# Who copies the triangular blocks: GpSimd alone, or VectorE and GpSimd

## The chip, the cores and the metric

One core of a Trainium2 chip runs the whole kernel; the seven others are idle. The metric is the device time of one execution in microseconds (us). The engines are PE (TensorE, with its weight loads as PEld), DVE (VectorE), ACT (ScalarE), POOL (GpSimd) and SP (SyncE, which issues the DMAs). Each runs its own list of instructions in order, and they wait for each other through semaphores.

## The reference

One layer of a streaming encoder over 1024 tokens of width 1024: a projection, four mixers side by side (gMLP, gated deltanet, rwkv7, a conformer convolution), an output projection, a gated feed-forward block and a gate by position. Everything is in float32. Two of the mixers are recurrences over time. The deltanet is written in chunks of 64 tokens and solves a triangular system in each:

```python
L = jnp.where(strict, jnp.einsum('bhnid,bhnjd->bhnij', kb, k) * decay, 0.0)
eye = jnp.eye(CHUNK, dtype=jnp.float32)
rhs = jnp.concatenate([v * beta[..., None], kb * jnp.exp(g)[..., None]], axis=-1)
sol = lax.linalg.triangular_solve(eye + L, rhs, left_side=True, lower=True)
```

The rwkv mixer is a recurrence token by token:

```python
sa = jnp.einsum('bhij,bhj->bhi', state, a_t)
state = (state * w_t[:, :, None, :] + sa[..., None] * b_t[:, :, None, :]
         + v_t[..., None] * k_t[:, :, None, :])
```

## The kernel before

Tokens lie in 8 tiles of 128 (two chunks of 64), and each mixer has 4 heads. The kernel brings the rwkv recurrence to the same chunked form as the deltanet, so both need the inverses of 64 (8 tiles x 2 chunks x 4 heads) unit triangular matrices of 64x64. The matrices of all tiles are inverted together, and that splits each mixer's work into three stages.

**Pass 1** (`deltanet_pass1`, `rwkv_pass1`) makes the triangular matrices tile by tile. In the deltanet a tile goes from PE through ACT and DVE into the SBUF tile `la` (L736), in rwkv from PE through one ACT copy for each half of the heads into `LT` (L1027), of which there are two buffers. Then `compact` copies the blocks of that tile out: the four diagonal 32x32 blocks, one in each group of 32 partitions, into `Cd` (`rCd` for rwkv, L1179), with the tile's number innermost, and the two blocks beside the diagonal into `Mo` (`rMo`, L1182). That is four copies and two copies of 32 partitions x 128 elements for a tile, all on POOL. The names `Cd`, `la`, `Mo` of the profile belong to the deltanet, `rCd`, `LT`, `rMo` to rwkv.

**Inversion.** When all 8 tiles have been copied, DVE transposes `Cd` into `Cs` (L741; `rCs`, L1031) and runs a substitution of 31 steps over all blocks at once (`invert`, L216 and L220), about 118 small DVE instructions. `blocks` then transposes the result twice (`Tc`, `Tn`, L1135 and L1137), and PE multiplies the blocks together (L1146, L1148).

**Tile loop.** The tiles are solved and the states carried on (`deltanet_tiles`, `rwkv_tiles`). At its start `expand` spreads the inverted blocks over a block matrix with copies of the same shape (L1190, L1192), for the first tile on DVE, for the others on POOL.

Around these stages PE has work that doesn't depend on them: during the deltanet's inversion the projections of the rwkv inputs (`rwkv_in`, L136, taken out by ACT at L190 and DVE at L195), during rwkv's pass 1 the last of those projections and two sums (L1007, which DVE multiplies at L1008), during rwkv's inversion the output projection of two finished mixers (`wout_early`, L136 with `osph` and `ospl`). DVE and ACT prepare that work's operands: a weight is cast by ACT (`wh`, L109) and its rest subtracted by DVE (`wl`, L112).

The order on each engine is set when the kernel is built: a scheduler places the instructions by priorities that the code sets and by modelled times. The order is then fixed.

Of the kernel before, what the change touches and what calls it, by code (L numbers as in the profile page):

```python
# [97 lines left out]
class Net:  # L98
# [591 lines left out]
    def deltanet_pass1(self, ip):  # L690
        tc, nc, I = self.tc, self.nc, self.i
        V, A, PO = nc.vector, nc.scalar, nc.gpsimd
        beta, nbeta, gr, Gc, nG, eG, beG, edk, tmp, tmp2 = [self.bsc[:, j, :] for j in range(10)]
        fl = lambda x: x.rearrange("p a b -> p (a b)")
        inv = lambda n: self.dt(n, [P, 32, 32])
        Cd = inv("Cd")
        Mo = [ip.tile([P, 16, 32], F32, name=f"Mo{g}") for g in range(2)]
        rs = self.brs
        cc = [slice(0, 64), slice(64, 128)]
        for t in range(NT):  # L700
            qt, kt = self.qt[t // 4][:, t % 4, :], self.kt[t // 4][:, t % 4, :]
            for x, r0 in ((qt, 0), (kt, 4)):
                xv = x.rearrange("p (h d) -> p h d", d=64)
                PO.tensor_tensor(out=xv, in0=xv, in1=rs[:, t, r0:r0 + 4, None].broadcast_to([P, H, 64]), op=ALU.mult)
            ps = self.mps("b")
            for pr in range(2):
                nc.tensor.transpose(ps[:, (2 * pr) * P:(2 * pr + 1) * P], kt[:, pr * P:(pr + 1) * P], self.ident)
                nc.tensor.transpose(ps[:, (2 * pr + 1) * P:(2 * pr + 2) * P], qt[:, pr * P:(pr + 1) * P], self.ident)
            kq = self.at("kq", [P, 4, P])
            A.copy(out=kq.rearrange("p a b -> p (a b)"), in_=ps)  # L710
            pd = self.mps("c")[:, 0:256].rearrange("p (h i) -> p h i", h=H)
            nc.tensor.matmul(pd, self.identb, self.negb[:, None, :].broadcast_to([P, H, 64]), start=True, stop=False)
            for h in range(H):
                for c in cc:
                    nc.tensor.matmul(pd[c, h, :], gr[:, t * 4 + h:t * 4 + h + 1].broadcast_to([P, 64]), self.incl[:, c],
                                     start=False, stop=h == H - 1)
            dq = self.at("dq", [P, 4, G])
            dT = dq[:, 0, :].rearrange("p (h i) -> p h i", h=H)
            V.tensor_tensor(out=dT, in0=pd, in1=nG[:, 4 * t:4 * t + 4, None].broadcast_to([P, H, 64]), op=ALU.add)
            A.activation(out=dT, in_=dT, func=AF.Exp)  # L720
            qe, qeT = dq[:, 1, :], dq[:, 2, :]
            PO.tensor_tensor(out=qe.rearrange("p (h d) -> p h d", d=64), in0=qt.rearrange("p (h d) -> p h d", d=64),
                             in1=eG[:, 4 * t:4 * t + 4, None].broadcast_to([P, H, 64]), op=ALU.mult)
            pq = self.mps("b")
            for pr in range(2):
                nc.tensor.transpose(pq[:, pr * P:(pr + 1) * P], qe[:, pr * P:(pr + 1) * P], self.ident)
            A.copy(out=qeT, in_=pq[:, 0:256])
            nc.sync.dma_start(out=self.d_qe[:, t, :], in_=qeT)
            la = self.at("la", [P, 2, H, 64])
            for hp in range(2):  # L730
                pk = self.mps("c").rearrange("p (r k i) -> p r k i", r=2, k=4)[:, :, 0:2, :]
                rw = slice(64 * hp, 64 * hp + 64)
                for pr in range(2):
                    for c in cc:
                        nc.tensor.matmul(pk[c, pr], kq[rw, 2 * pr, c], kq[rw, 2 * pr:2 * pr + 2, c], start=True, stop=True)
                V.tensor_tensor(out=la[:, :, hp::2, :].rearrange("p k r i -> p r k i"), in0=pk,  # L736
                                in1=dT[:, hp::2, None, :].broadcast_to([P, 2, 2, 64]), op=ALU.mult)
            nc.sync.dma_start(out=self.d_at[:, t, :], in_=la[:, 1].rearrange("p h i -> p (h i)"))
            self.compact(Cd, Mo, la[:, 0], t)
        Cs = inv("Cs")  # L740
        V.transpose(out=fl(Cs), in_=fl(Cd))  # L741
        bt = ip.tile([P, 32], F32, name="bt")
        V.transpose(out=bt, in_=beta)
        V.tensor_tensor(out=Cs, in0=Cs, in1=bt[:, :, None].broadcast_to([P, 32, 32]), op=ALU.mult)
        X = self.invert(inv, Cs, 1)
        return self.blocks(inv, X, Mo, ip.tile([P, 32, 32], F32, name="Tc"), nbeta, "bc")
# [265 lines left out]
    def rwkv_pass1(self, eA, bk):  # L1012
        nc, V = self.nc, self.nc.vector
        inv = lambda n: self.at2(n, [P, 32, 32])
        Cd = inv("rCd")
        Mo = [self.ip.tile([P, 16, 32], F32, name=f"rMo{g}") for g in range(2)]
        for t in range(NT):
            LT = self.ar.tile([P, H, 64], F32, name="LT", tag="LT", bufs=2)
            for hp in range(2):
                rw = slice(64 * hp, 64 * hp + 64)  # L1020
                pa = self.mps("a")[:, 0:P].rearrange("p (r i) -> p r i", r=2)
                for pr in range(2):
                    for c in range(2):
                        o = t * P + 64 * c
                        nc.tensor.matmul(pa[64 * c:64 * c + 64, pr, :], bk[pr][rw, t, 3 * c, :], eA[pr][rw, o:o + 64],
                                         start=True, stop=True)
                nc.scalar.copy(out=LT[:, hp::2, :], in_=pa)  # L1027
            self.compact(Cd, Mo, LT, t)
        fl = lambda x: x.rearrange("p a b -> p (a b)")
        Cs = inv("rCs")  # L1030
        V.transpose(out=fl(Cs), in_=fl(Cd))  # L1031
        X = self.invert(inv, Cs, -1)
        return self.blocks(inv, X, Mo, self.ip.tile([P, 32, 32], F32, name="rTc"), None, "ac")
# [137 lines left out]
            nc.vector.tensor_copy(out=outs[1].rearrange("p a b c -> p (a b c)"), in_=pU[64:128])  # L1171
        yield

    def compact(self, Cd, Mo, LT, t):
        PO = self.nc.gpsimd
        for b in range(4):
            bs = slice(32 * b, 32 * b + 32)
            o = 32 * (b % 2)
            PO.tensor_scalar(out=Cd[bs, :, 4 * t:4 * t + 4].rearrange("p i u -> p u i"), in0=LT[bs, :, o:o + 32],  # L1179
                             scalar1=1.0, scalar2=0.0, op0=ALU.mult, op1=ALU.add)  # L1180
        for c in range(2):
            PO.tensor_scalar(out=Mo[t // 4][64 * c:64 * c + 32, 4 * (t % 4):4 * (t % 4) + 4, :], in0=LT[64 * c:64 * c + 32, :, 32:64],  # L1182
                             scalar1=1.0, scalar2=0.0, op0=ALU.mult, op1=ALU.add)
# [456 lines left out]
```

## Time and profile before

| | us |
|---|---|
| median of 3 runs | 1516.09 (1514.38 to 1516.21) |
| the profiled execution's own time | 1511.95 |
| its span, first to last instruction | 1509.9 |
| PE busy | 1397.1 |
| DVE busy | 1022.3 |
| ACT busy | 606.2 |
| POOL busy | 499.6 |

The profiled execution lies 4.14 us under the median of the runs, and 2.05 us of its time lie outside the span. PE is busy 93% of the span, so an engine beside it matters where PE waits for it. Busy time of PE also depends on the clock that it was granted (PEclk, as a share of full speed). A wait is listed with the engine whose instruction ended it. The timeline puts neighbouring instructions of the same kind into one row (x4), whose duration is then that of all of them.

### The profile page before, as it was taken

The page shows a single profiled execution, that of the slowest core. Times are in us where ns is not written, and L with a number is a line of the kernel's source. Part 1 is how long each engine was busy: PE and PEld are TensorE (multiplying, and loading weights), DVE is VectorE, ACT ScalarE, POOL GpSimd, SP SyncE. Part 2 cuts the span into 40 slices and gives each one's busy share as a digit, 9 for nine tenths or more (in the row PEclk, how much of TensorE's full clock was granted, in tenths as well). Part 3 has the DMA queues.
Part 4 walks back from the last instruction along what each step waited for, and adds up shares of the span by engine and source line. Part 5 has one row for each costly group of instructions (what it writes and reads, how often), then busy time and mean ns, then how long its engine had stood idle before and what let it go on. Part 6 is the DMA issues. An engine that isn't in the chain of part 4 may idle for free.

```text
span 1509.9 us, 21011 instructions
## 1 busy us (share of the span) xinstructions
PE 1397.1 (93%) x7840; PEld 1112.8 (74%) x7840; DVE 1022.3 (68%) x1714; ACT 606.2 (40%) x998; POOL 499.6 (33%) x484
## 2 busy tenths in 40 slices
PE   7997998899996898998789999999999899998997
PEld 6885776677764676776667888888888778876785
DVE  5699853976565757667488676666665695777543
ACT  6352355122542233345453333333333334445535
POOL 3215236262335233123522222222221354574000
PEclk9997999989998799999899999999999999999999
DMA  6100113132144343223444332222233893373022
GB/s 218 61 29 28 60 52 127 56 89 60 56 171 147 107 137 106 71 94 133 145 144 171 105 103 91 91 92 94 97 103 110 268 308 110 102 259 126 27 99 97
DMA packets 91735, 171.76 MB, mean 114 GB/s; under 512 B 12401, under 2 KB 41713, under 8 KB 91377
## 3 DMA queue, kind: packets, MB, share of 16 engines
q1 hardware_dynamic: 91344, 169.93, 34.0%
q8 instruction: 61, 1.00, 0.3%
q10 hardware_dynamic: 288, 0.49, 0.1%
q14 instruction: 42, 0.34, 0.1%
HBM read 120.85 MB, written 49.55 MB: 113 GB/s over the span
## 4 chain that ended last, share of the span: by engine, by line
PE 42%; DVE 4%; issue 3%; DMA 3%; POOL 2%; ACT 1%; SPq 0%; DVEq 0%; POOLq 0%; ACTq 0%
PE pf L136 39%; DMA w<-in_wd 2%; POOL wl L1215 1%; PE mps L136 1%; PE px L136 1%; DVE w L1211 1%; DVE wl L1215 0%; PE pf L1556 0%; DVE t L1211 0%; DVE nxn L151 0%; DMA d_f<-fo 0%; DMA early<-in_wd 0%; DVE s L1211 0%; POOL t L1211 0%; DVE ys L1211 0%
## 5 line engine op out<-in xcount | busy, mean ns | idle before, releaser
L136 PE MATMUL mps<-hT,wh 128*128 128x512 f32 (+1 forms) x736 | 242.5, 409 | 4.2 <-DVE mix L195 2.5
L136 PEld LDWEIGHTS mps<-hT,wh 128*128 128x128 f32 x736 | 141.2, 198 | 37.9 <-DVE mix L195 2.9
L136 PE MATMUL mps<-hT,wl 128*128 128x512 f32 (+1 forms) x368 | 149.5, 406 | 3.2 <-POOL wl L112 3.2
L1215 POOL TENSOR_TENSOR wl<-yr,wh 128x512 fp32r<-128x512 f32 x73 | 106.4, 1463 | 99.6 <-ACT wh L1214 81.7
L136 PE MATMUL pf<-wh 128*128 128x512 f32 x300 | 118.4, 395 | 4.2 <-ACT wh L1214 4.2
L112 POOL TENSOR_TENSOR wl<-raw,wh 128x1024 fp32r<-128x1024 f32 x25 | 64.7, 2592 | 173.1 <-ACT wh L109 173.1
L136 PE MATMUL pf<-wl,wh 128*128 128x512 f32 x300 | 118.7, 396 | 3.3 <-DVE wl L1215 3.3
L136 PE MATMUL pf<-wh,wl 128*128 128x512 f32 x300 | 117.9, 393 | 0.0
L1211 DVE TENSOR_TENSOR pf<-pf,u 128x512 f32<-128x512 f32 x88 | 61.1, 694 | 70.9 <-PE pf L136 70.8
L1214 ACT CAST fq<-s 128x512 fp32r<-128x512 f32 x88 | 53.5, 620 | 121.6 <-PE pf L136 96.5
L1215 POOL TENSOR_TENSOR fq<-raw,fq 128x512 fp32r<-128x512 f32 (+1 forms) x31 | 50.2, 1620 | 153.9 <-ACT fq L1214 153.9
L1215 DVE TENSOR_TENSOR wl<-w,wh 128x512 fp32r<-128x512 f32 x62 | 70.3, 1140 | 40.7 <-ACT wh L1214 40.7
L567 DVE SCALAR_TENSOR_TENSOR cy<-csg,prmt,cy 128x1023 f32<-128x1023 f32 (+29 forms) x60 | 86.4, 1461 | 7.2 <-ACT cy L564 6.6
L1215 POOL TENSOR_TENSOR wl<-raw,wh 128x1024 fp32r<-128x1024 f32 (+1 forms) x17 | 40.4, 2378 | 142.1 <-issue 116.0
L136 PEld LDWEIGHTS mps<-hT,wl 128*128 128x128 f32 x368 | 72.3, 196 | 19.9 <-POOL wl L112 3.7
L1214 ACT CAST wh<-yr 128x512 fp32r<-128x512 f32 x73 | 45.1, 620 | 81.3 <-POOL wl L1215 49.2
L136 PEld LDWEIGHTS pf<-wl,wh 128*128 128x128 f32 x300 | 57.1, 190 | 17.7 <-DVE wl L1215 6.0
L136 PEld LDWEIGHTS pf<-wh 128*128 128x128 f32 x300 | 57.1, 191 | 16.6 <-ACT wh L1214 4.6
L1215 DVE TENSOR_TENSOR fq<-s,fq 128x512 fp32r<-128x512 f32 x66 | 45.6, 693 | 30.7 <-ACT fq L1214 30.7
L136 PEld LDWEIGHTS pf<-wh,wl 128*128 128x128 f32 x300 | 57.0, 190 | 11.7
L136 PE MATMUL pf<-xT2h,fq 128*128 128x512 f32 x176 | 60.1, 403 | 5.3 <-ACT fq L1214 5.3
L109 ACT CAST wh<-raw 128x1024 fp32r<-128x1024 f32 x30 | 31.4, 1046 | 72.6 <-PE mps L136 38.5
(484 smaller groups left out, 3619.8 us busy)
## 6 DMA issues: line engine op xcount, KB each, us to landing
yr<-d_y SPq DMA_DIRECT2D x73, 256.0 KB, 3.1
w<-in_wd SPq DMA_DIRECT2D x55, 256.0 KB, 4.2
raw<-in_wg SPq DMA_DIRECT2D x24, 512.0 KB, 3.7
raw<-in_wu SPq DMA_DIRECT2D x24, 512.0 KB, 3.5
raw<-in_win SPq DMA_DIRECT2D x22, 512.0 KB, 3.8
d_y<-fy SPq DMA_DIRECT2D x11, 512.0 KB, 3.5
d_y<-ys SPq DMA_DIRECT2D x11, 512.0 KB, 3.5
d_y<-ys SPq DMA_DIRECT2D x22, 256.0 KB, 3.9
```

Source lines behind the costliest of these rows:

```text
L109: self.nc.scalar.copy(out=hi, in_=raw)
L112: (eng or self.nc.vector).tensor_sub(out=lo, in0=raw, in1=hi.bitcast(F32))
L136: mm = lambda *a, **k: self.nc.tensor.matmul(*a, skip_group_check=more, **k)
L567: nc.vector.scalar_tensor_tensor(out=yc[:, sh:], in0=gl[:, 0:S - sh], scalar=self.prm("cfw", 2 * j + c), in1=yc[:, sh:], op0=ALU.mult, op1 ...
L1211: eng.tensor_tensor(out=out, in0=a, in1=b, op=op)
L1214: self.nc.scalar.copy(out=hi, in_=raw)
L1215: eng.tensor_sub(out=lo, in0=raw, in1=hi.bitcast(F32))
```

## The change

`compact` gets a number `nv`. The first `nv` of the four diagonal copies go to DVE, the others stay on POOL. The deltanet passes 2, rwkv passes 4. The copies beside the diagonal stay on POOL in both.

```diff
--- before.py
+++ after.py
@@ -736,7 +736,7 @@
                 V.tensor_tensor(out=la[:, :, hp::2, :].rearrange("p k r i -> p r k i"), in0=pk,
                                 in1=dT[:, hp::2, None, :].broadcast_to([P, 2, 2, 64]), op=ALU.mult)
             nc.sync.dma_start(out=self.d_at[:, t, :], in_=la[:, 1].rearrange("p h i -> p (h i)"))
-            self.compact(Cd, Mo, la[:, 0], t)
+            self.compact(Cd, Mo, la[:, 0], t, 2)
         Cs = inv("Cs")
         V.transpose(out=fl(Cs), in_=fl(Cd))
         bt = ip.tile([P, 32], F32, name="bt")
@@ -1025,7 +1025,7 @@
                         nc.tensor.matmul(pa[64 * c:64 * c + 64, pr, :], bk[pr][rw, t, 3 * c, :], eA[pr][rw, o:o + 64],
                                          start=True, stop=True)
                 nc.scalar.copy(out=LT[:, hp::2, :], in_=pa)
-            self.compact(Cd, Mo, LT, t)
+            self.compact(Cd, Mo, LT, t, 4)
         fl = lambda x: x.rearrange("p a b -> p (a b)")
         Cs = inv("rCs")
         V.transpose(out=fl(Cs), in_=fl(Cd))
@@ -1171,12 +1171,12 @@
             nc.vector.tensor_copy(out=outs[1].rearrange("p a b c -> p (a b c)"), in_=pU[64:128])
         yield
 
-    def compact(self, Cd, Mo, LT, t):
+    def compact(self, Cd, Mo, LT, t, nv):
         PO = self.nc.gpsimd
         for b in range(4):
             bs = slice(32 * b, 32 * b + 32)
             o = 32 * (b % 2)
-            PO.tensor_scalar(out=Cd[bs, :, 4 * t:4 * t + 4].rearrange("p i u -> p u i"), in0=LT[bs, :, o:o + 32],
+            (self.nc.vector if b < nv else PO).tensor_scalar(out=Cd[bs, :, 4 * t:4 * t + 4].rearrange("p i u -> p u i"), in0=LT[bs, :, o:o + 32],
                              scalar1=1.0, scalar2=0.0, op0=ALU.mult, op1=ALU.add)
         for c in range(2):
             PO.tensor_scalar(out=Mo[t // 4][64 * c:64 * c + 32, 4 * (t % 4):4 * (t % 4) + 4, :], in0=LT[64 * c:64 * c + 32, :, 32:64],
```

The scheduler places the moved copies, and a few neighbours move with them. On DVE, in rwkv's pass 1, from the last rwkv inputs to the start of the inversion (`mix_4092` and `mix_4156` are the two halves of the product of L1008, `mix_4284` and `mix_4320` two rwkv inputs):

```order
-L1008 TENSOR_TENSOR mix_4092<-mps,mix_4284 128x512 x2
+L1008 TENSOR_TENSOR mix_4092<-mps,mix_4284 128x512
+L1179 TENSOR_SCALAR rCd<-LT 32x4x32 x8
+L1008 TENSOR_TENSOR mix_4092<-mps,mix_4284 128x512
+L1179 TENSOR_SCALAR rCd<-LT 32x4x32 x4
 L1008 TENSOR_TENSOR mix_4156<-mps,mix_4320 128x512
 L112 TENSOR_TENSOR wl<-raw,wh 128x1024
+L1179 TENSOR_SCALAR rCd<-LT 32x4x32 x20
 L1031 STREAM_TRANSPOSE rCs<-rCd 128x1024
 L205 MEMSET X 128x1024
-L112 TENSOR_TENSOR wl<-raw,wh 128x1024
 L195 SCALAR_TENSOR_TENSOR mix_4320<-mps,prmt,mix_4320 128x511
```

The 32 copies stand between the first product of L1008 and the transpose, and the copies of tiles 3 to 7 stand behind the weight's L112. One `wl` has moved behind L195.

On ACT, in the same place:

```order
 L190 ACTIVATE mix_4284<-mps,omu 128x512
 L1027 COPY LT<-mps 128x2x64 x6
+L109 CAST wh<-raw 128x1024
+L1027 COPY LT<-mps 128x2x64 x2
 L1009 ACTIVATE mix_4092<-mix_4092,prmt 128x1024
-L109 CAST wh<-raw 128x1024
-L1027 COPY LT<-mps 128x2x64 x10
+L1027 COPY LT<-mps 128x2x64 x8
```

The cast of the weight that DVE's L112 takes now stands ahead of the copies of tile 3 and ahead of L1009.

On POOL, in the deltanet's pass 1, one tile (L722 makes the scaled queries `dq` of a later tile):

```order
 L722 TENSOR_TENSOR dq<-qt_1114,bsc 128x256 x2
-L1179 TENSOR_SCALAR Cd<-la 32x4x32 x4
+L1179 TENSOR_SCALAR Cd<-la 32x4x32 x2
 L1182 TENSOR_SCALAR Mo_1796<-la 32x128 x2
 L722 TENSOR_TENSOR dq<-qt_1114,bsc 128x256
```

Two of the four copies have left POOL's list, the rest of the list is in its old order. On DVE the two copies stand right behind the two L736 that write `la`, ahead of the next tile's L719.

## Rows read from the trace of the kernel before

**Rows 1.** Page, part 1: busy us, share of the span, instructions.
```profile
PE 1397.1 (93%) x7840; PEld 1112.8 (74%) x7840; DVE 1022.3 (68%) x1714; ACT 606.2 (40%) x998; POOL 499.6 (33%) x484
```

**Rows 2.** Busy us by stretch: length, PE, PEld, DVE, ACT, POOL, then PEclk, DMA, GB/s.
```profile
236.60:260.20 23.60, 20.62 (x286) 14.47 (x285) 8.27 (x21) 10.55 (x23) 20.61 (x52) 1.00 0.36 122
...
448.00:469.50 21.50, 14.46 (x135) 8.82 (x135) 2.97 (x5) 7.97 (x21) 17.86 (x46) 0.76 0.49 176
...
475.30:515.00 39.70, 31.44 (x122) 24.04 (x121) 38.02 (x131) 10.38 (x21) 12.97 (x5) 0.89 0.47 157
```

**Rows 3.** Waits, 447 to 476: who <- whom, us in total, times, longest.
```profile
DVE rCs L1031 <- POOL rCd L1179: 14.7, 1, 14.7
ACT LT L1027 <- POOL rMo L1182: 11.6, 6, 3.0
...
PE mps L1025 <- ACT LT L1027: 5.8, 5, 2.4
```

**Rows 4.** Timeline of PE: start, us, instructions [idle before <- releaser].
```profile
297.58 1.20 PE L1146 MATMUL mps<-Tn,Mo 32*32 32x32 f32 x64 [3.02 <-DVE Tn L1137]
...
473.60 0.80 PE L136 MATMUL mps<-wh,osph 128*128 128x512 f32 x1 [4.32 <-DVE mix L195]
...
515.17 1.92 PE L1146 MATMUL mps<-Tn,rMo 32*32 32x32 f32 x64 [3.70 <-DVE Tn L1137]
```

**Rows 5.** Groups by line, 448 to 470: busy us, mean ns | idle before <- releaser.
```profile
L1179 POOL TENSOR_SCALAR rCd<-LT 32x128 f32<-32x128 f32 x32 | 13.8, 431 | 18.5 <-issue 16.4
...
L1008 DVE TENSOR_TENSOR mix<-mps,mix 128x512 f32<-128x512 f32 x3 | 2.0, 687 | 1.8 <-PE mps L1007 1.8
```

**Rows 6.** Timeline of VectorE, the rwkv pass.
```profile
447.76 1.28 DVE L1008 TENSOR_TENSOR mix<-mps,mix 128x512 f32<-128x512 f32 x2
...
453.55 1.22 DVE L112 TENSOR_TENSOR wl<-raw,wh 128x1024 fp32r<-128x1024 f32 x1 [2.04 <-ACT wh L109]
...
469.49 1.25 DVE L1031 STREAM_TRANSPOSE rCs<-rCd 128x1024 f32<-128x1024 f32 x1 [14.72 <-POOL rCd L1179]
...
475.33 0.26 DVE L216 TENSOR_TENSOR Xt<-rCs,X 128x15 f32<-128x15 f32 x2
```

**Rows 7.** Lines 1190 and 1192 on VectorE: duration ns min/median/max, first and last start.
```profile
L1190 DVE TENSOR_SCALAR bbdT<-Tc x4: 293/514/517, 311.7 to 313.1; 32x128 f32<-32x128 f32 x4
...
L1190 DVE TENSOR_SCALAR sbdT<-rTc x4: 314/323/329, 530.4 to 531.5; 32x128 f32<-32x128 f32 x4
...
L1192 DVE TENSOR_SCALAR sbdT<-rMo x2: 316/1358/2401, 531.8 to 532.2; 32x128 f32<-32x128 f32 x2
```

**Rows 8.** Timeline of VectorE, 530 to 532.
```profile
530.40 1.38 DVE L1190 TENSOR_SCALAR sbdT<-rTc 32x128 f32<-32x128 f32 x4
```

**Rows 9.** Timeline of GpSimd, 529 to 535.
```profile
529.72 1.63 POOL L1190 TENSOR_SCALAR sbdT<-rTc 32x128 f32<-32x128 f32 x4
...
532.13 2.35 POOL L425 TENSOR_TENSOR h<-stg,h 128x1024 f32<-128x1024 f32 x1
```

**Rows 10.** Timeline of GpSimd, one tile of the deltanet pass.
```profile
249.38 1.82 POOL L1179 TENSOR_SCALAR Cd<-la 32x128 f32<-32x128 f32 x4
251.26 0.64 POOL L1182 TENSOR_SCALAR Mo<-la 32x128 f32<-32x128 f32 x2
251.99 0.61 POOL L722 TENSOR_TENSOR dq<-qt,bsc 128x256 f32<-128x256 f32 x1
```

**Rows 11.** Timeline of VectorE, the deltanet pass.
```profile
238.87 0.76 DVE L736 TENSOR_TENSOR la<-mps,dq 128x256 f32<-128x256 f32 x2 [0.66 <-ACT dq L720]
...
241.42 0.76 DVE L736 TENSOR_TENSOR la<-mps,dq 128x256 f32<-128x256 f32 x2 [0.71 <-ACT dq L720]
242.88 0.43 DVE L719 TENSOR_TENSOR dq<-mps,bsc 128x256 f32<-128x256 f32 x1 [0.71 <-POOL Mo L1182]
...
257.08 0.76 DVE L736 TENSOR_TENSOR la<-mps,dq 128x256 f32<-128x256 f32 x2 [1.29 <-ACT dq L720]
260.26 1.25 DVE L741 STREAM_TRANSPOSE Cs<-Cd 128x1024 f32<-128x1024 f32 x1 [2.43 <-POOL Cd L1179]
```

## The prediction

> **What bounds the kernel now.** I read the busy times first: PE is busy 93% of the span [rows 1], so moving work between two other engines pays only where PE waits for them. Then I looked for those places by stretch. In rwkv's pass 1, from 448.0 to 469.5, PE has 14.46 us of work in 21.50 us, at a granted clock of 0.76, while POOL is busy 17.86 us and DVE 2.97 us [rows 2]. In the deltanet's pass 1, from 236.6 to 260.2, POOL is busy 20.61 of 23.60 us and DVE 8.27 [rows 2]. The waits of the rwkv pass name the cause: DVE sits 14.7 us before the transpose of `rCd`, ended by POOL's copies; ACT waits 11.6 us in six pieces to write `LT` again, ended by POOL's copies beside the diagonal; PE waits 5.8 us for ACT [rows 3]. It is one ring: with two `LT` buffers, tile t+2 starts when POOL is done with tile t. Behind pass 1 the chain is closed too: during the inversion DVE is busy 38.02 of 39.70 us [rows 2], and PE waits for its result, `Tn`, at the end of both inversions, 3.02 us at 297.58 and 3.70 us at 515.17 [rows 4]. So what the transposes of `Cd` and `rCd` gain arrives at PE, and behind those points the instruction order is the old one: later stages can only shift.
>
> **What a copy costs.** On POOL a diagonal copy takes 0.43 us (13.8 us for 32) [rows 5]. On DVE this copy with its transposed output does not occur before. The nearest row is `expand` for the first tile of rwkv: four copies of the same size, one for each group of 32 partitions, 1.38 us together, so 0.345 each from start to start [rows 8], 0.314 to 0.329 long [rows 7], and they ran beside POOL copies of the same kind (529.72 to 531.35) [rows 9], as the new ones will. I take 0.345, the row that is like the new copies in size, partitions and neighbour. The bounds: 0.24 from below, an estimate for neighbours that overlap, from two instructions of the inversion that take 0.26 together at 15 elements [rows 6] with 0.1 added to each for 128 elements; and 0.51 from above, the median of the same copies in the deltanet's `expand` [rows 7], where POOL was busy with other kinds of work.
>
> **rwkv.** Removed from POOL: 32 copies, 13.8 us; what stays are two copies of 0.32 a tile (by the deltanet's row, 0.64 for two) [rows 10], which finish beside DVE's four. The order puts DVE's work in one line: two products of L1008 (1.28), a third (0.69), the weight's L112 (1.22) [rows 5, 6], and 32 x 0.345 = 11.04, together 14.2 us from 447.76. Is DVE fed? Tile t+2 needs one ACT copy pair behind DVE's copies of tile t, while DVE does tile t+1 for 1.38 us. ACT has 7.97 us of work in this stretch [rows 2], and the cast that now stands ahead of tile 3 should find its weight loaded, since the two weight buffers are refilled as DVE's L112 frees them and this is the older of the two. So DVE doesn't starve, and `rCd` is complete at 447.76 + 14.2 = 462.0 instead of 469.49 [rows 6]: 7.5 us earlier. From the transpose to the first step of the substitution DVE needs 5.84 us (469.49 to 475.33) [rows 6] for the same instructions in another order. The one among them that PE feeds is L195. By the new order eight matmuls of L136 stand behind PE's last tile, which ACT lets start at about 458.5; at 0.4 us each they end near 462, before DVE has done the transpose (1.25 us from 462.0) [rows 6] and the zeroing of X, so DVE finds its input ready. L195 moves ahead of one L112, and PE's wait of 4.32 us for it at 473.60 [rows 4] mostly goes: PE is some 8.7 us early there, and gives 1.2 of it back at `Tn`, where DVE sets the time. Term: **-7.5 us**.
>
> **Deltanet.** POOL's round for a tile is 1.82 + 0.64 + 0.61 us, 3.07 with small gaps to add [rows 10], and it sets the pace from the fourth tile on. With two copies fewer it is 2.16. What is late next is the loop of DVE, ACT and PE through L719, the exponential and L736: the one round in which POOL was not in the way took 2.55 us (238.87 to 241.42) [rows 11]. DVE's two copies (0.69) go into the gap between L736 and the next L719, 0.71 us [rows 11]; I add 0.1 for what sticks out. Six rounds of 2.65 from 238.87 put the last L736 at 254.8 instead of 257.08. Behind it POOL is no longer a tile late: half of 1.82 us follows the end of L736, so `Cd` is complete at 254.8 + 0.76 + 0.9 = 256.5 instead of 260.26 [rows 10, 11]. Term: **-3.8 us**. The bounds: with 0.51 a copy, 0.31 more sticks out, the round is 2.96, DVE's copies end last and the gain is 1.8 (2.2 in rwkv, where DVE's line is then 19.5 us; 4.0 together, 1512.1); with 0.24, nothing sticks out, the round stays 2.55 and the gain is 4.4. During this inversion DVE's L195 has had its input for some microseconds, so it doesn't wait.
>
> **The sum.** 7.5 + 3.8 = 11.3 us off the profiled execution: its span from 1509.9 to 1498.6, its own time from 1511.95 to 1500.65. The median of the runs lies 4.14 us above that time; I carry the offset along: 1516.1 - 11.3 = **1504.8 us**.
>
> **The rivals.** *The port is fought over.* A DVE copy beside POOL can cost more than itself: one of the copies of L1192 took 2.401 us instead of 0.316 [rows 7], and it ended together with a POOL instruction of 2.35 us that had just begun [rows 9]. If each of the 16 remaining `rMo` copies holds DVE up for its 0.32 us, rwkv loses 5.1 of its 7.5; in the deltanet each pair of DVE copies waits about 0.45 for a POOL copy in between, the round is 3.08 and the gain 1.0. Together 3.4: 1512.7 us. For it: that row. Against it: the copies of rows 8 ran beside four POOL copies and were not drawn out. The Trainium skill states it as a rule, in "SBUF — State Buffer", section "Who interferes with whom": a copy-like VectorE instruction in a two-port mode and a GpSimd instruction exclude each other for their whole length, and the second one blocks. The row of 2.401 us agrees; the rows of rows 8 and 9 do not show it.
>
> *Better than the estimate.* At 0.24 a copy DVE's line in rwkv is 3.2 + 7.7 = 10.9 us, `rCd` is complete at 458.7, 10.8 us early, if ACT keeps up; with 4.4 in the deltanet 15.2: 1500.9 us.
>
> *The gain is hidden.* PE's own filling work could become the bound behind the transposes. PE is 2.3 us early at the end of the deltanet's pass, and has 3.02 us of wait to lose, 5.3 together, so it covers 3.8; in rwkv 8.7 and 3.70 cover 7.5. It would take a longer stretch at a low clock behind `Tn`, as the 0.76 of the rwkv pass [rows 2] shows one, brought on by a longer wait. Then within 3 us of 1516.1.
>
> *Slower.* The transposed write, a step of 32 elements between neighbours, may be dear on DVE. On POOL the same copy costs 0.43 against about 0.32 for the plain one, a ratio of 1.34; with it DVE's would be 0.46, and a wait of 0.32 for POOL on each makes 0.78: 32 x 0.78 + 3.2 = 28.2 us, 6.5 late in rwkv, and a deltanet round of 2.55 + 0.85 = 3.4, which ends 1.3 late. Together 7.8 slower: 1523.9 us. In rwkv alone it decides above (21.73 - 3.2) / 32 = 0.58 us a copy; POOL has only 16 copies to wait for, so 0.78 for all 32 is more than they can cause.
>
> **How the numbers follow.** Forecast 0.55, fought port 0.21, better 0.10, hidden 0.08, slower 0.06. A measurement of this kernel can tell about 0.2%, 3 us. Faster by more than that: 0.55 + 0.10 + two thirds of the fought port, 0.14 = 0.79. Within it: 0.08 + 0.07 = 0.15. Slower: 0.06. The range goes from the better case, 1500.9, to just above the fought port's 1512.7: 1500.5 to 1513.2, which leaves out the slower and hidden cases and a little of the better one.
>
> **What would show it.** In the changed profile: DVE's groups of `rCd` copies at 1.4 us a tile (at 2 us the port is fought over, at 1 us they overlap); `rCs` at 462 and `Cs` at 256.5; ACT's wait for POOL's `rMo` gone; POOL idle for most of rwkv's pass; PE still waiting for `Tn` at both inversions. I am wrong if DVE waits between its copies, if ACT's cast or PE's matmuls feed it late, or if `Tn` comes early and PE, busy with its filling work, doesn't take it.

## The result, and the profile after

| | kernel before | changed kernel |
|---|---|---|
| median, us | 1516.15 (1514.38 to 1529.06, 4 executions) | 1499.31 (1497.17 to 1507.29, 4 executions) |
| ratio, 95% interval | | 0.9888 [0.9839, 0.9937] |
| profiled execution: own time, span | 1511.95, 1509.9 | 1500.98, 1499.2 |

The kernel is faster by about 1.1%: by 16.8 us between the medians and by 10.97 us between the two profiled executions; 11.3 us were forecast. In some executions of both kernels PE's granted clock falls a second time early in rwkv's tile loop (their mean granted clock is 0.953 or less, that of the others 0.956 or more), and these are some 15 to 20 us longer than the rest.

Page of the changed kernel, busy times (as rows 1):

```profile
PE 1393.3 (93%) x7840; PEld 1112.0 (74%) x7840; DVE 1038.4 (69%) x1762; ACT 606.1 (40%) x998; POOL 480.7 (32%) x436
```

48 instructions left POOL, 48 came to DVE; PE's share is the old one. By stretch (length, then PE, PEld, DVE, ACT, POOL, PEclk, DMA, GB/s), the deltanet's pass from its first `la` to `Cs` and rwkv's from line 1007 to `rCs`, of the changed kernel:

```profile
235.70:256.30 20.60, 20.60 (x284) 15.51 (x284) 14.32 (x40) 10.30 (x22) 14.40 (x36) 1.00 0.44 147
442.10:458.10 16.00, 13.72 (x146) 8.11 (x146) 15.44 (x41) 7.43 (x21) 5.67 (x16) 0.92 0.69 255
```

The same stretches took 24.5 and 24.2 us before. In the first PE is now busy all the time; in the second DVE is, 15.44 of 16.00 us, where it had sat idle behind POOL [rows 2, 3]. DVE's timeline of the changed kernel in rwkv's pass (start, us, instructions, as rows 6):

```profile
444.57 0.69 DVE L1008 TENSOR_TENSOR mix<-mps,mix 128x512 f32<-128x512 f32 x1
445.23 2.76 DVE L1179 TENSOR_SCALAR rCd<-LT 32x128 f32<-32x128 f32 x8
...
451.62 6.44 DVE L1179 TENSOR_SCALAR rCd<-LT 32x128 f32<-32x128 f32 x20
458.10 1.25 DVE L1031 STREAM_TRANSPOSE rCs<-rCd 128x1024 f32<-128x1024 f32 x1
...
460.34 0.63 DVE L195 SCALAR_TENSOR_TENSOR mix<-mps,prmt,mix 128x511 f32<-128x511 f32 x1
...
463.89 0.26 DVE L216 TENSOR_TENSOR Xt<-rCs,X 128x15 f32<-128x15 f32 x2
```

Nothing in this line waits: 20 copies in 6.44 us, 0.322 each, and 0.326 over all 32 (2.76 + 1.22 + 6.44 us). `rCs` starts 11.4 us earlier than before, `rCs` to the first step of the substitution is 5.8 us as before. DVE's timeline of the changed kernel in the deltanet's pass (as rows 11):

```profile
241.28 0.76 DVE L736 TENSOR_TENSOR la<-mps,dq 128x256 f32<-128x256 f32 x2 [0.61 <-ACT dq L720]
242.07 0.67 DVE L1179 TENSOR_SCALAR Cd<-la 32x128 f32<-32x128 f32 x2
...
243.85 0.76 DVE L736 TENSOR_TENSOR la<-mps,dq 128x256 f32<-128x256 f32 x2 [0.64 <-ACT dq L720]
...
256.28 1.25 DVE L741 STREAM_TRANSPOSE Cs<-Cd 128x1024 f32<-128x1024 f32 x1 [0.38 <-POOL Cd L1179]
```

The round is 2.57 us (241.28 to 243.85) and the transpose waits 0.38 us for POOL where it waited 2.43 [rows 11]. The copies one by one, from the changed kernel's groups by line (duration in ns, min/median/max):

```profile
L1179 DVE TENSOR_SCALAR rCd<-LT x32: 262/290/406, 445.2 to 457.8; 32x128 f32<-32x128 f32 x32
L1179 DVE TENSOR_SCALAR Cd<-la x16: 267/334/394, 236.5 to 255.5; 32x128 f32<-32x128 f32 x16
L1179 POOL TENSOR_SCALAR Cd<-la x16: 402/408/514, 236.6 to 255.8; 32x128 f32<-32x128 f32 x16
L1182 POOL TENSOR_SCALAR rMo<-LT x16: 287/291/892, 445.3 to 456.7; 32x128 f32<-32x128 f32 x16
```

The transposed write is no dearer on DVE than expected. POOL's longest copy of rwkv's pass, 892 ns from 450.96 on, ran not beside the moved copies but beside the weight's L112 on DVE (450.49 to 451.71), and POOL has time. PE's waits of the changed kernel at the places of rows 4, and one more, at 500.34:

```profile
293.86 1.20 PE L1146 MATMUL mps<-Tn,Mo 32*32 32x32 f32 x64 [1.58 <-DVE Tn L1137]
...
461.02 0.74 PE L136 MATMUL mps<-wh,osph 128*128 128x512 f32 x2 [1.53 <-DVE mix L195]
...
500.34 0.80 PE L136 MATMUL mps<-wh,ospl 128*128 128x512 f32 x1 [4.23 <-DVE ospl L112]
504.42 1.81 PE L1146 MATMUL mps<-Tn,rMo 32*32 32x32 f32 x60 [3.28 <-DVE Tn L1137]
```

PE takes the first `Tn` 3.7 us and the second 10.75 us earlier and still waits for both, so the gain of the passes, 12.1 us together, reaches it but for 1.3 us.

### The profile page after: what moved, and what is told of

The parts are those of the page before. It is cut to its first block, busy times and chain, and to the rows that moved or that the text cites. A ratio compares the mean times of both kernels' runs of the same rounds, so it can differ in the third digit from the quotient of the medians.

```text
span 1499.2 us, 21025 instructions
## 1 busy us (share of the span) xinstructions
PE 1393.3 (93%) x7840; PEld 1112.0 (74%) x7840; DVE 1038.4 (69%) x1762; ACT 606.1 (40%) x998; POOL 480.7 (32%) x436
## 4 chain that ended last, share of the span: by engine, by line
PE 43%; DVE 3%; issue 3%; DMA 2%; POOL 2%; ACT 1%; SPq 0%; DVEq 0%; POOLq 0%; ACTq 0%
PE pf L136 40%; DMA w<-in_wd 1%; POOL wl L1215 1%; PE mps L136 1%; PE px L136 1%; PE pf L1556 0%; DVE t L1211 0%; DVE wl L1215 0%; DVE nxn L151 0%; DMA raw<-in_wpg 0%; DVE w L1211 0%; DMA early<-in_wd 0%; DVE s L1211 0%; POOL t L1211 0%; DVE ys L1211 0%
## 5 line engine op out<-in xcount | busy, mean ns | idle before, releaser
L136 PE MATMUL mps<-hT,wl 128*128 128x512 f32 (+1 forms) x368 | 148.9, 405 | 4.9 <-POOL wl L112 4.9
L112 POOL TENSOR_TENSOR wl<-raw,wh 128x1024 fp32r<-128x1024 f32 x25 | 64.6, 2588 | 174.9 <-ACT wh L109 174.9
```

What stands on the lines that cost most here:

```text
L112: (eng or self.nc.vector).tensor_sub(out=lo, in0=raw, in1=hi.bitcast(F32))
L136: mm = lambda *a, **k: self.nc.tensor.matmul(*a, skip_group_check=more, **k)
```

## The experiments

**Theory at first:** the trace accounts for all of it, 11 us, and the rest is the spread of few executions. Its rival: the change is worth 16 us in truth, and something outside the two passes gains 5.

**e1: the changed kernel again, no edit,** with twelve executions.

> The changed kernel once more, beside the kernel before, in more executions. Theory A, the trace accounts for all of it: profiled against profiled the span fell by 10.7 us (1509.9 to 1499.2), so the ratio is about 0.993 and the larger difference of the medians (16.8 us, 0.989) was the spread of single executions (1497.2 to 1507.3 after, 1514.4 to 1529.1 before). Theory B, the change saves some 5 us more than its profiled execution shows: the ratio stays at 0.989.

Median 1499.34 against 1515.05 (30 executions), ratio 0.9936 [0.9902, 0.9969]. Both theories get half: the interval agrees with 11 us, the medians differ by 15.7. The twelve are in two clusters, eight from 1497.3 to 1505.6 and four from 1514.9 to 1527.1 (the upper cluster), so that interval mostly counts how many fell in which. The profiled one is from the upper cluster, and it shows what that is. By stretch, e1 first:

```profile
510.00:520.00 10.00, 10.00 (x105) 7.95 (x103) 6.53 (x14) 2.98 (x7) 7.15 (x13) 0.79 0.66 191
520.00:530.00 10.00, 8.62 (x45) 6.08 (x44) 2.36 (x4) 1.99 (x5) 2.17 (x6) 0.55 0.54 165
530.00:540.00 10.00, 10.00 (x76) 8.44 (x76) 3.35 (x7) 2.27 (x6) 1.74 (x5) 0.50 0.13 38
540.00:550.00 10.00, 10.00 (x48) 7.46 (x46) 2.09 (x7) 2.82 (x7) 2.48 (x7) 0.50 0.10 30
550.00:560.00 10.00, 10.00 (x79) 8.11 (x80) 4.55 (x18) 1.64 (x4) 0.41 (x1) 0.50 0.22 69
```

And the changed kernel's first profile:

```profile
510.00:520.00 10.00, 10.00 (x133) 8.06 (x128) 4.29 (x10) 2.96 (x6) 4.38 (x9) 0.50 0.32 95
520.00:530.00 10.00, 9.43 (x74) 6.70 (x73) 5.54 (x9) 2.95 (x8) 4.63 (x9) 0.99 0.70 196
530.00:540.00 10.00, 10.00 (x112) 8.11 (x112) 4.91 (x12) 4.16 (x12) 2.92 (x9) 1.00 0.41 135
```

Same program, and e1 was even 3.2 us earlier at the second `Tn`. Then in e1 the granted clock, which was back at 1.00 from 515.1 to 519.1, falls to 0.50 (1.2 of 2.4 GHz) and stays there until about 565 while PE is busy all the time; from `Tn` to the end e1 takes 1014.0 us instead of 996.9. At that point PE waits, in e1 and in the first profile:

```profile
521.52 1.12 PE L1078 MATMUL mps<-ident,rbk 128*128 128x128 f32 x4 [1.38 <-DVE rAA L1071]
```

```profile
525.19 0.66 PE L1078 MATMUL mps<-ident,rbk 128*128 128x128 f32 x4 [0.57 <-DVE rAA L1071]
```

**e2, e3: each half of the change alone** (e2 has the first edit, e3 the second).

```diff
-            self.compact(Cd, Mo, la[:, 0], t, 2)
+            self.compact(Cd, Mo, la[:, 0], t, 0)
```

```diff
-            self.compact(Cd, Mo, LT, t, 4)
+            self.compact(Cd, Mo, LT, t, 0)
```

> Only rwkv's 32 copies on VectorE, the deltanet's all on GpSimd. Theory A: the transpose of rCd comes 8.2 us earlier by its own pass (it came 11.4 earlier, 3.2 of which had come from the deltanet), so about 7.5 us off, ratio 0.995; Cs as before at 260.3. Theory B, a gain elsewhere: more than 10 us off with this half alone, or none.

> Only the deltanet's 16 copies on VectorE, rwkv's all on GpSimd. Theory A: Cs at 256.3 instead of 260.3, and 3.2 us off the end, ratio 0.998; GpSimd's wait in rwkv's pass as before, 14.7 us ahead of rCs. If the two halves help each other (the rival to a plain sum), this run gains nothing by itself: its 3.2 us would be eaten by rwkv's pass.

rwkv alone 1503.93, ratio 0.9939 [0.9914, 0.9963]; the deltanet alone 1509.35, 0.9991 [0.9950, 1.0032], with five of its twelve executions in the upper cluster. Their profiles give the pieces apart: e2 has rwkv's pass at 16.2 us and the deltanet's at 24.4, e3 24.2 and 20.6. Each half is worth in its place what it is worth in the whole. Without the upper clusters e2 is 10 and e3 7 us below the kernel before, more than the 7.5 and 3.2 expected.

**e4: rwkv's copies for two tiles in one instruction** (half as many on either engine, twice as long).

```diff
+            if t % 2 == 0:
+                L2 = self.ar.tile([P, 2 * H, 64], F32, name="LT", tag="LT", bufs=2)
+            LT = L2[:, 4 * (t % 2):4 * (t % 2) + 4]
...
-            self.compact(Cd, Mo, LT, t, 4)
+            if t % 2:
+                self.compact(Cd, Mo, L2, t // 2, 4, 8)
...
```

> rwkv's triangular blocks copied for two tiles at once: 16 copies of 256 elements instead of 32 of 128 on VectorE, 8 instead of 16 on GpSimd. A copy is mostly fixed cost (0.29 us for 128 elements), so by theory A 16 copies of about 0.40 us, 6.4 instead of 9.9 us, and rCs 2 to 3.5 us earlier than in the changed kernel: 2 to 3 us faster than it. Rival: the pass is by now fed by ACT and PE, and waiting for two tiles costs what the fewer copies save: same as the changed kernel within 1 us.

DVE's timeline of e4:

```profile
448.13 5.65 DVE L1182 TENSOR_SCALAR rCd<-LT 32x256 f32<-32x256 f32 x12
453.82 1.25 DVE L1034 STREAM_TRANSPOSE rCs<-rCd 128x1024 f32<-128x1024 f32 x1
```

A copy of 256 elements takes 0.471 us, two of 128 take 0.652; the pass is 13.7 us instead of 16.0, as expected. The time is not: median 1502.03, 0.9917 [0.9886, 0.9949], no better than the changed kernel. Its profiled execution gives the 2.3 us back between `rCs` and `Tn` (45.9 us in e4, 43.2 and 44.2 in the first two profiles of the changed kernel). Why that piece varies by 2 us is the question of e7 and of e13 to e16; the scatter of the times comes first.

**e5, e6: PE's wait in front of line 1078 filled,** in the changed kernel and in the one before.

```diff
+            if t == 0:
+                pw = self.mps("c"); self.rot -= 1
+                for _ in range(6):
+                    nc.tensor.transpose(pw[:, 0:P], bk[:, 0, 0, :], self.ident)
             ps = self.mps("a")
```

> The changed kernel with six extra transposes on PE in rwkv's tile loop, first tile only, ahead of those of line 1078; their result is not used, so about 1.6 us of PE work at full clock is added and nothing left out. Behind Tn, PE waits there for DVE's rAA of line 1071: 0.6 us in the four profiled executions whose granted clock stayed at 1.00 afterwards, 1.4 us in the two in which it fell to 0.50 at that point and stayed for some 40 us. Theory A (the spread of single executions comes from that wait: the clock falls where PE pauses there): the wait is below 0.5 us, no second fall, no execution with a mean clock under 0.956, all between 1495 and 1508, median 1498. Theory B (the clock falls there for another reason, such as the load before): filling the wait changes nothing, one execution in three or four has 40 us at 0.50 behind line 1078 and takes 1514 or more.

> The kernel before with the same six extra transposes, nothing left out. Theory A: no execution over 1520, where 5 of 30 of the kernel before took 1525 or more; median 1511 to 1513. Against it the run of the changed kernel with the same transposes is 9 to 11 us less, which is what the two profiles and a comparison at equal mean clock give, not 16.8 as the first medians. Theory B: still one in six at 1525 or more, and the difference of the medians as it falls out, 6 to 17.

e5: median 1497.57 (1494.94 to 1500.96), 0.9859 [0.9819, 0.9900]. e6: 1515.13 (1508.56 to 1517.29), 0.9975 [0.9949, 1.0001]. None of the 18 executions is in the upper cluster; without the fill 13 of 70 executions of the kernel before (4 of the 23 that ran beside e5 and e6) and 4 of 16 of the changed one are. e8 and e11, in whose profiles PE doesn't wait in front of line 1078 either, have none in 22. PE's timeline of e5 shows the filled place:

```profile
522.18 0.77 PE L1078 MATMUL mps<-ident,rbk 128*128 128x128 f32 x5
523.42 0.66 PE L1082 MATMUL mps<-ident,rbk 128*128 128x128 f32 x4 [0.47 <-DVE rAA L1071]
```

So the second fall goes with PE's pause there, and filling the pause takes it away (Theory A). But with it removed from both, the change is worth 17.6 us by the medians and 16.1 by the means, not the expected 9 to 11. The first theory has fallen: the second fall accounts for the two clusters, not for the missing 5 us.

**e7: wout's partial results added by DVE from PSUM,** not staged by ACT and added by POOL.

```diff
-                for _ in self.wout_tile(t, ofs, w, len(ms) == 2):
+                for _ in self.wout_tile(t, ofs, w):
```

> The changed kernel, in which wout's partial results in the inversions are added to h by DVE straight from PSUM (line 427) and no longer by ACT's copy and POOL's addition (lines 423 and 425). In the trace of the changed kernel five of DVE's steps of the rwkv inversion take 2.25 to 2.6 us where their neighbours of the same size take 0.2 to 0.5; each begins while a POOL addition of line 425 (2.34 to 3.26 us) runs, and ends with it. Theory A (the two engines exclude each other for the length of that POOL instruction): the five long steps are gone, DVE has some seven additions of 0.69 more in the inversion, the way from rCs to Tn (line 1137) is 39 to 41 us instead of 44.2, and the kernel is 3 to 5 us faster than the changed one, 1494 to 1496. Theory B (the steps are long for another reason): five long steps stay, the additions come on top, the way is 49 us, 1503.

Median 1485.02 (1478.75 to 1497.03), 0.9795 [0.9747, 0.9844]: 14 us less than the changed kernel, where 3 to 5 were expected. The substitution's steps of line 216 in the rwkv inversion, in the changed kernel and in e7 (ns, min/median/max):

```profile
L216 DVE TENSOR_TENSOR Xt<-rCs,X x59: 170/264/2449, 463.9 to 497.5; 128x110 f32<-128x110 f32 x5, 128x120 f32<-128x120 f32 x5, 128x126 f32<-128x126 f32 x5, 128x56 f32<-128x56 f32 x4
```

```profile
L216 DVE TENSOR_TENSOR Xt<-rCs,X x59: 170/257/295, 464.7 to 497.6; 128x110 f32<-128x110 f32 x5, 128x120 f32<-128x120 f32 x5, 128x126 f32<-128x126 f32 x5, 128x56 f32<-128x56 f32 x4
```

The long steps are gone, and `rCs` to `Tn` takes 41.0 us instead of 44.2: the POOL additions had made them. The Trainium skill states this in "SBUF — State Buffer", section "Who interferes with whom": "A DVE instruction with two SBUF inputs contends with a GpSimd instruction that reads SBUF"; the traces agree, at 2.0 to 2.3 us a time here. The larger part of e7's gain lies behind `Tn`: from the second `Tn` to the end its profile takes 980.9 us, the changed kernel's 996.9. Between the second `Tn` and the feed-forward block PE has less of wout left to do. PE's groups by line there, changed kernel and e7:

```profile
L136 PE MATMUL mps<-wh,ospl 128*128 128x512 f32 x53 | 24.9, 470 | 0.0
```

```profile
L136 PE MATMUL mps<-wh,ospl 128*128 128x512 f32 x43 | 19.1, 443 | 0.0
```

Ten matmuls fewer, and ten and eleven in the two sister groups (`wl,osph` and `wh,osph`, 53 to 43 and 42): 31 x 0.46 = 14 us that were done in front of `Tn`, where PE had been waiting. This part is no price of long steps alone, since the edit also takes the copies of line 423 from ACT. Two of e7's six executions, 1496.2 and 1497.0, lie 9 us and more above the other four, so its median is known to a few us only.

**e8: rwkv's DVE copies issued twice.**

```diff
+            for _ in range(2 if nv == 4 else 1):
```

> The changed kernel with each of DVE's 32 copies in rwkv's pass issued twice, the second with the same result; 32 more DVE instructions, nothing left out. Theory A (DVE's line is the bound of the pass, and what is gained or lost there reaches the end): 32 x 0.29 = 9.3 us, rCs 9 to 10 us later than in the changed kernel (16.0 us from line 1007 to rCs become 25 to 26), and the time 8 to 10 us longer, 1507, about what the kernel with the deltanet's part alone has. Theory B (much of a shift of that pass is absorbed behind it, by PE's filling work or the clock): the pass is longer by as much, the time by less than 4 us.

The pass is 30.2 us, 14 more instead of 9.3, since the longer line also let other DVE work in between (two weights and an `ospl` of line 112 and an L195 stand among the copies, some 3.7 us). The time is 1511.22 (1506.68 to 1514.08), 0.9957 [0.9930, 0.9985], 11.9 us over the changed kernel. What is lost in that pass reaches the end to more than four fifths; "hidden" is out.

**e9, e10: e7's edit together with those of e4 and e5, and e7's edit in the kernel before.**

> The changed kernel with three edits that have run apart from each other: wout's partial results added by DVE from PSUM, copies of two tiles in one instruction in rwkv's pass, and the six extra transposes on PE in front of line 1078. Theory A (the gains lie at different places and add up): rCs 13.7 us behind line 1007 instead of 16.2, no POOL addition in the rwkv inversion, so 2 to 3 us less than with the additions on DVE alone (1485.0): 1482 to 1483, and no execution above 1490. Theory B (the pass is no longer what the end waits for once the inversion is shorter): 1485 again.

> The kernel before with wout's partial results added by DVE from PSUM, POOL's additions of line 425 gone. Theory A (the exclusion between DVE and those POOL additions costs the kernel before the same as the changed one): no DVE step over 2 us in the rwkv inversion but those beside other POOL work, from rCs to Tn 40 to 41 us instead of 43.5 to 45.4, and 13 to 15 us less than the kernel before, 1501 to 1503; the change is then worth 16 us beside it (1485.0 against 1501). Theory B (the gain of those additions needs the earlier rCs): less than 8 us, above 1508.

e9: 1487.20 (1482.32 to 1494.02), 0.9788 [0.9729, 0.9846], the same as e7; its pass is 13.7 us, but nothing comes of it, and two of its six executions are above 1490, which Theory A had excluded. The profiled one (1490.93) is one of them: in spite of the fill its granted clock is 0.50 from about 512 to 542 us, with PE busy all the time, behind a pause of PE of 1.25 us at line 1060. It takes 992.9 us from `Tn` to the end, e7 980.9, so e9 doesn't show whether the gains add up. e10: 1494.62 (1492.44 to 1499.53), 0.9837 [0.9780, 0.9894], 18.8 us below the kernel before and 6 below the least that Theory A expected. Beside e10 the change is worth 9.6 us by e7's median, less than the 16 expected. By the ratios to the kernel before (0.9795 and 0.9837, from different rounds) it is some 6 us, and their intervals overlap: that the change gains less where POOL's additions don't reach DVE is not shown.

**e11: all of the deltanet's diagonal copies on DVE** (`nv` 4 in the first call).

> The changed kernel with all four diagonal copies of the deltanet's tiles on DVE too, POOL left with the Mo copies. A round of DVE is 2.55 us with a gap of 0.64. Theory A (the gap takes two more copies of 0.335, and POOL's are no longer waited for): the round stays 2.55 to 2.7, the pass from its first la to Cs 20.5 to 21.5 us against 20.6, the time within 2 us of the changed kernel. Theory B (DVE becomes the bound of the pass, since every round also has to wait for ACT's dq of 0.6 us that the gap is): round 3.2, pass 24 to 25, 3 to 5 us slower, the deltanet's whole gain gone.

DVE's timeline of e11:

```profile
248.99 0.76 DVE L736 TENSOR_TENSOR la<-mps,dq 128x256 f32<-128x256 f32 x2 [0.48 <-ACT dq L720]
249.78 1.65 DVE L1179 TENSOR_SCALAR Cd<-la 32x128 f32<-32x128 f32 x4
251.46 0.42 DVE L719 TENSOR_TENSOR dq<-mps,bsc 128x256 f32<-128x256 f32 x1
252.37 0.76 DVE L736 TENSOR_TENSOR la<-mps,dq 128x256 f32<-128x256 f32 x2 [0.48 <-ACT dq L720]
```

Theory B: the round is 3.38 us, the gap in front of L736 is ACT's answer to L719 and stays at 0.48 us, and the pass is 24.8 us, the old length. 1503.52, 0.9928 [0.9901, 0.9955], 4.2 us over the changed kernel. The profiled execution, the fastest of the ten (1493.91), doesn't show that loss: its rwkv pass took 14.0 us instead of 16.0, and its second `Tn` comes at 502.5. Of the two shares tried there, half is the better by the medians.

**e12: rwkv's `Mo` copies on DVE too,** POOL out of the pass.

```diff
-            PO.tensor_scalar(out=Mo[t // 4][64 * c:64 * c + 32, 4 * (t % 4):4 * (t % 4) + 4, :], in0=LT[64 * c:64 * c + 32, :, 32:64],
+            (self.nc.vector if nv == 4 else PO).tensor_scalar(out=Mo[t // 4][64 * c:64 * c + 32, 4 * (t % 4):4 * (t % 4) + 4, :], in0=LT[64 * c:64 * c + 32, :, 32:64],
```

> The changed kernel with rwkv's 16 Mo copies on DVE too, so that POOL is out of that pass. Theory A (DVE's line is the bound and its copies cost about the same beside POOL and without it): 16 x 0.29 = 4.6 us more, rCs 20 to 21 us behind line 1007 instead of 16.0; the copies of rCd at 0.26 to 0.30 as now. Theory B (the two engines fight over the port in that pass): the rCd copies get cheaper by over 0.1 us each, 3.2 us, and rCs comes at most 1.5 us later.

Groups by line (busy us, mean ns, as rows 5) of the changed kernel and of e12, and e12's copies (ns, min/median/max):

```profile
L1179 DVE TENSOR_SCALAR rCd<-LT 32x128 f32<-32x128 f32 x32 | 10.0, 311 | 0.5
```

```profile
L1179 DVE TENSOR_SCALAR rCd<-LT 32x128 f32<-32x128 f32 x32 | 9.0, 283 | 0.5
...
L1179 DVE TENSOR_SCALAR rCd<-LT x32: 265/283/301, 443.1 to 457.4; 32x128 f32<-32x128 f32 x32
L1182 DVE TENSOR_SCALAR rMo<-LT x16: 214/217/219, 444.3 to 457.9; 32x128 f32<-32x128 f32 x16
```

Without POOL beside them the `rCd` copies take 283 ns in the mean instead of 311 (in the median 283 instead of 290): that is what POOL's copies cost them in this pass, 32 x 0.028 = 0.9 us. The pass is 18.2 us, between the two expectations, since `Mo` is cheaper on DVE than thought and one product of L1008 has moved behind the pass. One execution, 1505.93.

**e13 to e16: two more profiles of each kernel, no edit,** for the missing 5 us.

> The kernel before, unchanged, for a second profiled execution of it. Theory A (the 4.1 us by which the first profiled execution lay under the median are steps of 2 us that it happened not to have): from Cs to Tn of the deltanet 37.3 us instead of 35.3, with a third DVE step of over 2 us beside a POOL subtraction of line 112, as in two of the other three profiles that have the old deltanet pass; from rCs to Tn 45 to 47 instead of 43.5; own time 1514 to 1516, with the two passes at 24.5 and 24.2 as before. Theory B (the offset lies elsewhere, behind Tn or around the span): 35.3 and 43.5 again, and 4 us more behind Tn.

> The same, for a third profiled execution of the kernel before: Theory A 37.3 and 45 to 47 in at least one of the two, own time in step with them; Theory B 35.3 and 43.5 in both, with the difference in own time behind Tn.

> The changed kernel, unchanged, for a third profiled execution. Theory A: the passes at 20.6 and 16.0, Cs to Tn 35.5, rCs to Tn 43 to 44, and so the sum of the pieces up to the second Tn 13 to 17 us less than in the typical execution of the kernel before. Theory B: 35.5 to 37.5 and 44 to 46 as often as in the kernel before, and the pieces up to Tn 12 us less.

> The same, for a fourth profiled execution of the changed kernel: Theory A 35.5 and 43 to 44 again; Theory B 37.5 or 45 and more.

Own times 1511.85, 1515.78, 1520.31 and 1497.89; e15 has the second fall (and waited 1.5 us in front of line 1078; the others 0.6 to 1.0). The pieces, in us, from the first starts of the instructions named (`Tn` as DVE's transpose), with e5 and e6, whose fill lies behind them:

| piece | before, e13, e14, e6 | mean | changed, e1, e15, e16, e5 | mean | difference |
|---|---|---|---|---|---|
| first `la` to `Cs` | 24.5, 24.4, 24.4, 24.6 | 24.5 | 20.6, 20.6, 20.6, 20.6, 20.6 | 20.6 | -3.9 |
| `Cs` to `Tn` | 35.4, 35.4, 37.3, 37.3 | 36.3 | 35.5, 35.4, 35.4, 35.4, 35.4 | 35.4 | -0.9 |
| `Tn` to line 1007 | 149.7, 148.1, 150.9, 151.1 | 149.9 | 150.3, 147.9, 150.0, 148.0, 148.2 | 148.9 | -1.0 |
| line 1007 to `rCs` | 24.2, 24.2, 24.2, 24.3 | 24.2 | 16.0, 16.0, 16.2, 16.0, 16.0 | 16.0 | -8.2 |
| `rCs` to `Tn` | 43.5, 46.2, 46.6, 45.5 | 45.5 | 44.2, 43.2, 47.1, 44.3, 44.2 | 44.6 | -0.9 |
| second `Tn`, from the start | 513.0, 514.6, 518.5, 518.0 | 516.1 | 502.3, 499.1, 504.8, 500.2, 500.5 | 501.4 | -14.7 |

The two passes repeat to 0.2 us and give 12.1; the other pieces move in steps of about 2 us. Such a step is, for one, a DVE instruction that meets a POOL one. At the end of the rwkv inversion, DVE and POOL of e13:

```profile
509.49 0.22 DVE L220 TENSOR_TENSOR X<-X,Xt 128x60 f32<-128x60 f32 x1
509.74 2.28 DVE L216 TENSOR_TENSOR Xt<-rCs,X 128x31 f32<-128x31 f32 x1
```

```profile
509.64 2.34 POOL L425 TENSOR_TENSOR h<-stg,h 128x1024 f32<-128x1024 f32 x1 [4.18 <-ACT stg L423]
```

And of the kernel before, the same instructions in its first profile:

```profile
509.86 0.19 DVE L216 TENSOR_TENSOR Xt<-rCs,X 128x31 f32<-128x31 f32 x1
...
510.53 1.95 DVE L1135 STREAM_TRANSPOSE rTc<-X 128x1024 f32<-128x1024 f32 x1
```

```profile
510.21 2.62 POOL L425 TENSOR_TENSOR h<-stg,h 128x1024 f32<-128x1024 f32 x1 [4.99 <-ACT stg L423]
```

There the fifth addition came when the last two-input step was done and fell beside a transpose, which has one input and was not drawn out (1.95 us, 1.92 in e13); in e13 it came 0.57 us earlier and cost 2.1 us. So the first profile of the kernel before had four such long steps in this inversion and two in the deltanet's. e13 had five and two, e14 five and three, e6 four and three (an `ospl` of line 112 counts where it takes over 2 us). The changed kernel has no fewer in this inversion, four in e1 and five in its other profiles, and two in the deltanet's.

A second kind of step is a wait of DVE for ACT's `osph`, on which an `ospl` in the substitution depends. PE and DVE of e13, and of the changed kernel's first profile:

```profile
472.57 0.80 PE L136 MATMUL mps<-wh,osph 128*128 128x512 f32 x1 [3.72 <-DVE mix L195]
473.16 0.63 PE L136 MATMUL mps<-wl,osph 128*128 128x512 f32 x1
...
478.76 0.43 DVE L112 TENSOR_TENSOR ospl<-oaf,osph 128x256 fp32r<-128x256 f32 x1 [1.80 <-ACT osph L109]
```

```profile
461.60 0.40 PE L136 MATMUL mps<-wl,osph 128*128 128x512 f32 x1
...
466.50 0.43 DVE L112 TENSOR_TENSOR ospl<-oaf,osph 128x256 fp32r<-128x256 f32 x1
```

In the four profiles of the first column PE waits 3.7 to 4.3 us for L195, the granted clock is 0.50 behind that wait, its matmuls take 0.63 instead of 0.40 us, and DVE waits 0.9 to 2.3 us. In the changed kernel PE waits 1.5 to 1.7 us there, and in four of five profiles the clock stays at 1.00 and DVE doesn't wait; in e15 the clock falls a little later and DVE waits 2.7 us. On average that is 1.2 us less in the changed kernel, enough for the 0.9 of `rCs` to `Tn`; no run changes this wait alone.

Theory A holds for e14. e13 has the 46.2 us but not the 37.3, and its own time is that of the first profile, not 1514 to 1516. For the changed kernel e15 goes against it with 47.1.

## Why the prediction was right or wrong

- **What bounds the kernel.** Right. The passes ended behind POOL's copies, and PE waits for both `Tn` before and after.
- **What a copy costs.** Right: 0.345 taken, 0.326 measured in rwkv, 0.335 in the deltanet, no wait between copies. The bounds of 0.24 and 0.51 were not reached.
- **rwkv's term.** Mechanism right, size 7.5 forecast, 8.2 measured. The line of DVE took 13.5 us from the first L1008 to `rCs` instead of 14.2, nearly all of it the 0.019 us less a copy. L195 found its input, and PE's wait of 4.32 us there is 1.53.
- **The deltanet's term.** 3.8 forecast, 3.9 measured; `Cs` at 256.28, forecast 256.5.
- **The sum on the profiled execution.** Own time 1500.65 forecast, 1500.98 measured. That it is so close is partly luck: the two passes gave 12.1 us instead of 11.3, and in this pair of executions 1.3 us of them were gone at the second `Tn`, in pieces between and behind the passes that differ by 2 to 4 us between executions of one kernel.
- **The step that failed: "The median of the runs lies 4.14 us above that time; I carry the offset along."** The offset belongs to that one execution and to a median of three, not to the kernel: the profiled execution of the changed kernel lies 1.7 us above its median, not 4.14 below. Of the 4.14 us, 2.0 were the small sample (the 57 executions of the kernel before without a second fall have a median of 1514.05). The profiled execution had the shortest `rCs` to `Tn` and the fewest long steps of four, and its second `Tn` came 3.0 us before their mean, but that doesn't settle the rest, since e13 has one step more and the same own time. Behind the offset stands "later stages can only shift": between and behind the passes the pieces were taken at the length that they had in one trace, and they moved by 2 to 4 us. With own time against own time the forecast is within 0.4 us, with the offset it is 5.5 us too long, 1.2 us beyond the low end of the range, which was made of the price of a copy and had no room for the scatter of single executions. The row of 2.401 us stood in the prediction [rows 7, 9], but as a price that a copy might pay, and it wasn't asked what else in the inversions pays it already.
- **The rivals.** The port is fought over, but little by the copies: 0.9 us in rwkv by e12, where the rival had 5.1. The 2 us go to DVE steps with two inputs in SBUF beside POOL's long instructions, six to eight of them in a profile of the kernel before and six or seven in the changed one's. Better than the estimate: no, 0.24 a copy did not occur. Hidden: no, more than four fifths of e8's loss came out. Slower: no.
- **What stays open.** From the 14.7 us at the second `Tn` to the 15.8 us between the medians of the executions without a second fall (1514.05 and 1498.21) 1.2 us are left. And of the 14.7, 2.8 lie in the pieces that move in steps. In `rCs` to `Tn` the meetings with POOL are not rarer in the changed kernel, but PE's shorter wait for L195 and the clock behind it can account for the 0.9 us. The 0.9 in `Cs` to `Tn` may be chance: e7 and e8 have the deltanet's new pass too, and 37.5 us there. The 1.0 in `Tn` to line 1007 is unexplained; nine executions can't tell whether the change causes it.

## What to carry to other kernels

A profiled execution is one draw: before its distance to a median is carried over, look for long instructions of a kind that is short elsewhere, and count how many of them that execution happened to have. Copies that hold up a pass can go to the engine that waits for them, up to the gap it has: in rwkv all, in the deltanet half. Where a serial chain of two-input VectorE steps sets the end, large two-input GpSimd work beside it is worth moving first; here that one line (e7) gave 14 us on top of the change, 3 of them in the chain itself, and is, at 1485.0 us, the fastest version with e9.

## What the runs showed of the hardware

- A GpSimd addition of 128x1024 in float32 takes 2.34 us and stops a VectorE instruction with both inputs in SBUF that starts during it: 2.28 us instead of 0.19. It also stopped a `TENSOR_SCALAR` copy, which has one input (2.401 us instead of 0.316 [rows 7, 9]). The transpose was not drawn out (1.95 us beside the addition, 1.92 without). `TENSOR_SCALAR` copies beside GpSimd copies of their own size took 0.311 us in the mean, without them 0.283.
- A pause of PE of 1.4 to 1.5 us in front of line 1078 went with a granted clock of 0.50 for some 40 us of full work in the three profiles that had it (e1, e2, e15), a pause of 0.6 to 1.0 us with none in the seven other profiles with that work in its old form (the kernel before, e3, e4, e13, e14, e16 and the changed kernel's first); it cost 17 to 18 us from `Tn` to the end (1013.4 to 1014.0 us against 995.4 to 996.9). Some 1.6 us of unused transposes on PE in that pause removed it in 18 executions (e5, e6). e9's profile, with the same transposes, has 0.50 for some 30 us of full work behind a pause of 1.25 us at another line.
- On VectorE a copy of 32x128 with a transposed write takes 0.326 us from start to start and one of 32x256 0.471, both beside GpSimd copies: by these two, an estimate, 0.18 us of it doesn't depend on the length.
